# The output projection's gate rows on the weights' queue, three of them moved among the projections, and the correction turned inside a value block

## The chip, the cores and the metric

The kernel runs on one core of a Trainium2 chip. Its engines work side by side and each goes through its own list of instructions in order: TensorE (PE) multiplies matrices and loads its weights on a second track (PEld), VectorE (DVE), ScalarE (ACT) and GpSimd (POOL) compute elementwise, SyncE (SP) only issues transfers (DMAs). A DMA can also be issued by another engine, here by POOL; it then stands in that engine's list. An instruction waits until what it reads is there and what it overwrites is free.

The metric is the device time of one execution in microseconds (us); lower is better. "Before" is the kernel as it was, "after" the changed one.

## What is computed

One layer of a diffusion backbone over 512 latent tokens and 256 context tokens, model width 2048, all in float32. The lines of the reference that the change's surroundings compute:

```python
mod_x = (silu(c) @ w_ada + b_ada)                 # 6 x 2048 modulation values for the latent tokens
sh1, s1, g1, sh2, s2, g2 = split(mod_x, 6)
h = modulate(rmsnorm(x, norm1_w), sh1, s1)        # and hc for the context
p = h @ w_in                                      # one input projection: q, k, v, c_q, c_kv, k_rope
...                                               # 8 heads of differential, 8 of latent attention
x = x + g1 * (merge_heads(o_da, o_mla) @ w_o)     # output projection, 2048 x 2048, gated by g1
h2 = modulate(rmsnorm(x, norm2_w), sh2, s2)
x = x + g2 * conv_ffn(h2, w_up, conv_w, conv_b, w_down)
return rmsnorm(x, final_w)
```

The modulation `silu(c) @ w_ada` is a matrix times one vector. Its 96 rows of 128 outputs are computed apart from each other: row j brings a 128 x 2048 tile of `w_ada` (1 MB) and makes column j of the tile `modx`. Columns 0 to 31 (shift and scale of the first norm) are made at the start, 32 to 47 are the gate g1, 48 to 79 the shift and scale of the second norm, 80 to 95 the gate g2. The 64 rows behind the first 32 are spread over later stages; they are called **gate rows** here.

## The kernel before

**Products.** Each float32 product is made of three passes (`mm3`, lines 103 to 109): both operands are split into a high and a low half, and PE adds high x high (L107), high x low (L108) and low x high (L109). A weight block is a 128 x 1024 raw tile `wr` (512 KB, one DMA on SP's queue, L89 in `wraw`). ACT copies its high half `wh` out (a cast), DVE subtracts that from `wr` to give the low half `wl`, and then PE can run the block. `wh` and `wl` have three buffers each.

**A gate row** (`gemv`, L169 to L176) is a DMA of 1 MB into a tile `ada` of two buffers, and one multiply-and-sum on DVE against the activated vector held in `cb`, which writes one column of `modx`. Whatever engine `queue` names issues the DMA; without one it is SP. The rows come from one iterator `gv` in the order 64 to 79, 32 to 47, 48 to 63, 80 to 95, and `next_gemv(pool, count, queue)` takes the next `count` of them, so a row placed earlier shifts all that follow.

**The projections** (about 120 to 437 us of the span) are 36 blocks in an order written out by hand (`manual_schedule`): what the program emits in turn is what each engine does in turn. `step(block, tasks)` emits the block's matmuls, then the cast of the block two ahead, the first task, the low half of the block two ahead, the load of the block four ahead, and the other tasks. Here `wr` has two buffers. Gate rows are tasks (`gemvs(1)`) and their DMAs go on POOL's queue (`gp`); 35 of the 64 rows are done in this stage.

Eight of the blocks make the values of the first four heads (`value_block`, called for n_ = 0 to 7 with the tasks of `plan[n_]`): six products of 128 x 512, one for each group of 128 tokens, summed over 16 tiles of the width. The last of them goes through its order group by group, 12 pairs of a group and a half of the weight block.

**The correction.** The first products of the projection are made before the shift of the modulation is known, and a bias `beta` is added to them later. Two rows of sums for it are collected in two PSUM tiles `ac` (named `b_1432` and `b_1433` below); `bias_turn` turns them from rows into columns by six small products with `sel` (printed as x4 and x2), and `bias_out` copies the columns to `beta` with two DVE copies, one of 8 and one of 4 columns. Before, `bias_turn` is called after the eight value blocks, and `bias_out` is the first task of the next step, `block(1, 0)`. That step's block writes its result in PSUM.

**The output projection** (about 822 to 1027 us) is a double loop: four groups of output columns, and in each eight weight blocks of `w_o`; a block feeds four products of 128 x 512 with two tiles of the attention's output each, 24 matmuls in all. Here a scheduler orders the instructions of each engine from the program's order and the buffers: `wr` has three buffers, `ada` two, `xr` three. Behind the eighth block of a group (run in the order of the outputs) come four outputs: a tile `xr` of x is loaded on SP, DVE forms `x + g1 * product` from column 32 + dt of `modx`, POOL issues the write of the result (`x_d`) and adds its square to `ss`. Before, a gate row on POOL's queue stands ahead of each block but the first three of the first group, 29 in all:

```python
for g in range(4):
    for kb in range(8):
        if g or kb > 2:
            next_gemv(wo, 1, gp)
        wh, wl = wblock(w_o[g, kb])
        ...
    for i in range(4):
        nc.sync.dma_start(xr, x_t[dt])
        ...
        gp.dma_start(x1_d[dt], x)
```

Behind it comes the gated MLP to the end of the program; the change leaves it as it is.

Of the kernel before, what the change touches and what calls it, by code (L numbers as in the profile page):

```python
# [52 lines left out]
def layer_kernel(ctx: ExitStack, tc: tile.TileContext, small, rope, c_row, cc_row, x_t, ctx_t, ada, ada_k,  # L53
# [484 lines left out]
    def gemvs(count):  # L538
        return lambda: next_gemv(sp_, count, gp)
# [129 lines left out]

    def value_block(half, vo, n_, last):  # L670
        wh, wl = hl_w.pop(len(steps))
        order = [(j, t) for t in last for j in range(2)] if n_ == 7 else [(j, t) for j in range(2) for t in range(NKEY)]
        for j, t in order:
            kt = KB[half][n_] * 2 + j
            w = (wh[:, j * 512:(j + 1) * 512], wl[:, j * 512:(j + 1) * 512])
            src, o = (hx[kt], t * P) if t < 4 else (hc[kt], (t - 4) * P)
            mm3(vo[t], (src[0][:, o:o + P], src[1][:, o:o + P]), w, n_ == 0 and j == 0, n_ == 7 and j == 1)
# [57 lines left out]
    with tc.manual_schedule(engines=every):  # L735
        raws[4] = keep(lat0[4], None, raw_query())
        for f in (2, 3, 0, 1):
# [15 lines left out]
                [lambda: add_shift([7], gemvs(1)), gemvs(1)],  # L753
                [gemvs(1), gemvs(1)], [gemvs(1), gemvs(1)])
        for n_ in range(8):
            step(lambda: value_block(0, v0, n_, first), *plan[n_])
            if 2 < n_ < 7:
                bias_products(n_ - 3)
        bias_turn()

# [27 lines left out]

        step(block(1, 0), bias_out, lay(0), lay(5), gemvs(1), lay(1, True), gemvs(1))
        step(block(1, 1), lay(2), lay(3), gemvs(1), lay(4, True))  # L790
        step(block(2, 0), gemvs(1), feature_keys(1))
# [14 lines left out]

        step(lambda: latent(0, 0), gemvs(1))
        step(lambda: latent(0, 1), feature_keys(6))
        step(lambda: latent(1, 0), gemvs(1), lambda: keep_cq(0))
        step(lambda: latent(1, 1), gemvs(1))  # L810
        step(lambda: latent(2, 0), gemvs(1), lambda: keep_cq(1))
# [285 lines left out]
    for g in range(4):  # L1097
# [5 lines left out]
        for kb in range(8):  # L1103
            if g or kb > 2:
                next_gemv(wo, 1, gp)
            wh, wl = wblock(w_o[g, kb])
            order = [(j, i) for j in range(2) for i in range(4)]
            for j, i in sorted(order, key=lambda t: t[1]) if kb == 7 else order:
                kt, o = kb * 2 + j, j * 512 + i * P
                mm3(outs[i], (wh[:, o:o + P], wl[:, o:o + P]), osp[kt], kt == 0, kt == 15)  # L1110
# [564 lines left out]
```

## Time and profile before

| | us |
|---|---|
| three runs | 2421.64, 2428.02, 2425.93 |
| median | 2425.93 |
| the profiled execution, its own time | 2423.42 |
| its span (first to last instruction in the trace) | 2421.6 |

The mean granted clock of TensorE in the profiled execution is 0.991 of full speed.

The windows of the profile over the stages, with busy time of each engine in us (instructions in brackets), the granted clock, the share of the DMA engines and GB/s:

```profile
120.00:437.00 317.00, 311.10 (x1557) 259.51 (x1557) 248.01 (x310) 89.27 (x134) 30.77 (x57) 0.98 0.73 264
437.00:822.00 385.00, 364.11 (x1885) 285.45 (x1883) 311.92 (x495) 215.18 (x413) 40.37 (x34) 1.00 0.35 105
822.00:1027.00 205.00, 191.88 (x836) 155.26 (x837) 140.74 (x142) 56.20 (x75) 42.42 (x55) 0.98 0.74 269
1027.00:2421.00 1394.00, 1369.05 (x7494) 1191.16 (x7492) 981.42 (x1207) 688.09 (x955) 161.82 (x188) 0.99 0.52 135
```

The columns behind the length are PE, PEld, DVE, ACT and POOL. A line of the timeline, further down, reads: start, duration, engine, line, operation, output <- inputs, shapes, count, and in square brackets the time that the engine had been idle and what released it. A busy PE may still be slow: its time at a lower clock counts as busy.

### The profile page before, as it was taken

Reading aid. Unit: us, or ns where it says so; the run is one execution under the profiler, and the core shown is the slowest. Engines: PE = TensorE matmul, PEld = TensorE weight load, DVE = VectorE, ACT = ScalarE, POOL = GpSimd, SP = SyncE. Lnnn points to the kernel's source line nnn. Section 1 sums busy time; section 2 is a strip of 40 time slices with the busy share of each in tenths; the row PEclk is TensorE's granted clock in tenths of the full one; section 3 lists DMA queues with packets and bytes.
Section 4 is the critical chain, followed back from the end, with each engine's and each line's share of the span. In section 5 each row is a group of like instructions: output and inputs, shape, how many; then the busy total and the mean of one; then the engine's idle time right before and its main releaser. Section 6 shows DMA issues by size and latency. Waiting matters only on the chain.

```text
span 2421.6 us, 32339 instructions
## 1 busy us (share of the span) xinstructions
PE 2342.4 (97%) x12444; PEld 1969.0 (81%) x12444; DVE 1774.9 (73%) x2303; ACT 1099.8 (45%) x1660; POOL 281.7 (12%) x350
## 2 busy tenths in 40 slices
PE   8999999999899998999999999999999999999997
PEld 5787888777677787788888888888888888888887
DVE  5996786698787877597576767676767676676667
ACT  5322322455555621254454545454445454454543
POOL 0001000121100022200101010101011111111113
PEclk9999999999999999999999999999999999999999
DMA  9767776853301289613555454545555555555572
GB/s 381 276 225 282 289 283 257 231 151 106 127 33 48 72 324 334 213 58 130 140 134 145 129 147 124 152 120 156 122 157 122 157 122 150 129 140 138 135 213 79
DMA packets 141514, 407.45 MB, mean 168 GB/s; under 512 B 14880, under 2 KB 31792, under 8 KB 130736
## 3 DMA queue, kind: packets, MB, share of 16 engines
q1 hardware_dynamic: 103552, 271.15, 34.1%
q0 software_dynamic: 36656, 133.19, 21.2%
q8 instruction: 97, 1.59, 0.3%
q10 hardware_dynamic: 1152, 1.05, 0.1%
q14 instruction: 57, 0.47, 0.1%
HBM read 335.86 MB, written 69.48 MB: 167 GB/s over the span
## 4 chain that ended last, share of the span: by engine, by line
PE 77%; DVE 9%; issue 7%; DMA 4%; ACT 3%; POOL 2%; SPq 0%; DVEq 0%; POOLq 0%; ACTq 0%
PE y L1373 13%; PE b L107 9%; PE b L108 9%; PE b L109 9%; PE z L1373 6%; PE y L1375 6%; PE z L1375 3%; PE s L881 3%; PE x L1373 2%; PE s L108 2%; PE s L107 2%; PE s L109 2%; DMA ada<-in_ada 1%; PE x L1375 1%; PE pt L893 1%
## 5 line engine op out<-in xcount | busy, mean ns | idle before, releaser
L1394 POOL DMA_DIRECT2D x_d<-xs x160 | 140.4, 1020 | 1165.4 <-ACT xs L1393 1135.7
L107 PE MATMUL b<-ah,wh 128*128 128x512 f32 (+1 forms) x672 | 259.3, 386 | 0.0
L108 PE MATMUL b<-al,wh 128*128 128x512 f32 (+1 forms) x672 | 259.2, 386 | 0.0
L109 PE MATMUL b<-ah,wl 128*128 128x512 f32 (+1 forms) x672 | 258.3, 384 | 0.0
L1349 DVE TENSOR_TENSOR wl<-wr,wh 128x1024 fp32r<-128x1024 f32 x126 | 153.9, 1221 | 128.9 <-ACT wh L1343 128.9
L1349 DVE TENSOR_TENSOR wl<-rb,wh 128x1024 fp32r<-128x1024 f32 x124 | 151.3, 1221 | 127.8 <-ACT wh L1343 127.8
L1343 ACT CAST wh<-wr 128x1024 fp32r<-128x1024 f32 x126 | 132.2, 1049 | 206.4 <-PE b L108 100.7
L1343 ACT CAST wh<-rb 128x1024 fp32r<-128x1024 f32 x124 | 130.2, 1051 | 189.8 <-PE b L108 115.8
L1349 DVE TENSOR_TENSOR wl<-ws,wh 128x1024 fp32r<-128x1024 f32 x123 | 150.1, 1221 | 88.7 <-ACT wh L1343 88.7
L1343 ACT CAST wh<-ws 128x1024 fp32r<-128x1024 f32 x123 | 128.3, 1043 | 137.9 <-PE b L108 45.2
L174 DVE CUSTOM_DVE_ANT_0 ada<-ada,cb,smt 128x2048 f32<-128x2048 f32 x64 | 153.3, 2397 | 50.3 <-DMA ada<-in_ada 50.2
L109 PEld LDWEIGHTS b<-ah,wl 128*128 128x128 f32 x672 | 126.4, 188 | 25.5
L107 PE MATMUL b<-a2k,wh 128*128 128x512 f32 (+1 forms) x352 | 135.7, 388 | 11.0 <-DVE beta L733 5.9
L107 PEld LDWEIGHTS b<-ah,wh 128*128 128x128 f32 x672 | 126.7, 188 | 22.9
L108 PEld LDWEIGHTS b<-al,wh 128*128 128x128 f32 x672 | 126.7, 189 | 21.9
L109 PE MATMUL b<-a2k,wl 128*128 128x512 f32 (+1 forms) x352 | 134.0, 381 | 6.3 <-DVE wl L81 6.3
L80 ACT CAST wh<-wr 128x1024 fp32r<-128x1024 f32 (+2 forms) x64 | 64.0, 1002 | 120.1 <-PE s L108 37.1
L210 ACT CAST wh<-wr 128x1024 fp32r<-128x1024 f32 x38 | 39.9, 1051 | 150.4 <-PE b L109 41.9
L1373 PE MATMUL y<-b2k,wh 128*128 128x512 f32 x410 | 106.9, 391 | 0.0
L883 DVE TENSOR_REDUCE m<-s 128x1 f32<-128x768 f32 x96 | 90.4, 950 | 22.6 <-PE s L881 22.2
L1393 ACT ACTIVATE xs<-b,modx 128x512 f32<-128x512 f32 x160 | 100.8, 680 | 0.3 <-DMA x_d<-xs 0.3
L81 DVE TENSOR_TENSOR wl<-wr,wh 128x1024 fp32r<-128x1024 f32 (+2 forms) x64 | 76.4, 1196 | 30.5 <-ACT wh L80 30.4
(536 smaller groups left out, 6113.7 us busy)
## 6 DMA issues: line engine op xcount, KB each, us to landing
ada<-in_ada POOLq DMA_DIRECT2D x80, 1024.0 KB, 5.9
rb<-in_w_up SPq DMA_DIRECT2D x123, 512.0 KB, 4.4
wr<-in_w_dn SPq DMA_DIRECT2D x84, 512.0 KB, 4.0
x_d<-xs POOLq DMA_DIRECT2D x160, 256.0 KB, 6.0
wr<-in_w_up SPq DMA_DIRECT2D x53, 512.0 KB, 4.3
wr<-in_w_f SPq DMA_DIRECT2D x34, 512.0 KB, 6.1
adak<-in_ada_k SPq DMA_DIRECT2D x64, 256.0 KB, 5.4
wr<-in_w_o SPq DMA_DIRECT2D x32, 512.0 KB, 5.4
```

The lines of the kernel that those rows point to most:

```text
L81: ve.tensor_tensor(dst_l, src, dst_h.bitcast(F32), op=ALU.subtract)
L107: pe.matmul(out, st[0], mv[0], start=start, stop=False, **kw)
L108: pe.matmul(out, st[0], mv[1], start=False, stop=False, **kw)
L109: pe.matmul(out, st[1], mv[0], start=False, stop=stop, **kw)
L174: ve.tensor_tensor_reduce(out=junk, in0=w, in1=vec, op0=ALU.mult, op1=ALU.add, scale=1.0, scalar=col("b_ada", j), accum_out=dst[:, j:j + 1])
L883: ve.tensor_reduce(out=m, in_=s[:, :TT], axis=AX.X, op=ALU.max, negate=True)
L1343: sc.copy(hi, raw)
L1349: ve.tensor_tensor(lo, raw, hi.bitcast(F32), op=ALU.subtract)
L1373: pe.matmul(o, w[j][0], hs[j], start=start and j == 0, stop=False, skip_group_check=True)
L1375: pe.matmul(o[:, h0], w[j][1], hs[j][:, h0], start=False, stop=j == 7, skip_group_check=True)
L1393: sc.mul(x, po, modx[:, 80 + dt:81 + dt])
L1394: gp.dma_start(x1_d[dt], x, accum_op=ALU.add)
```

## The change

Four things are done. (a) In the output projection the gate rows lose their queue argument, so that SP issues them in between the weights' loads, and the condition changes: the first group has its rows at kb 3 to 7 as before, the three others at kb 0 to 6, none ahead of their last block. That is 5 + 3 x 7 = 26 rows. (b) The three rows taken out there become tasks of three steps of the projections, behind `block(1, 1)`, `latent(0, 0)` and `latent(1, 1)`, on POOL's queue; 38 rows are done there then. As the iterator's order stays, each place behind the first of these works on a later row than it did. (c) `bias_turn` is called in the middle of the last first-value block, after six of its 12 pairs, no longer behind it. (d) `bias_out` is emitted between the two gate rows of that block's step, no longer as the first task of the step that follows.

```diff
-    def value_block(half, vo, n_, last):
+    def value_block(half, vo, n_, last, midway=None):
...
-        for j, t in order:
+        for k, (j, t) in enumerate(order):
+            if midway and k == len(order) // 2:
+                midway()
...
-                [gemvs(1), gemvs(1)], [gemvs(1), gemvs(1)])
+                [gemvs(1), gemvs(1)], [gemvs(1), bias_out, gemvs(1)])
         for n_ in range(8):
-            step(lambda: value_block(0, v0, n_, first), *plan[n_])
+            step(lambda: value_block(0, v0, n_, first, bias_turn if n_ == 7 else None), *plan[n_])
...
-        bias_turn()
...
-        step(block(1, 0), bias_out, lay(0), lay(5), gemvs(1), lay(1, True), gemvs(1))
-        step(block(1, 1), lay(2), lay(3), gemvs(1), lay(4, True))
+        step(block(1, 0), lay(0), lay(5), gemvs(1), lay(1, True), gemvs(1))
+        step(block(1, 1), lay(2), lay(3), gemvs(1), lay(4, True), gemvs(1))
...
-        step(lambda: latent(0, 0), gemvs(1))
+        step(lambda: latent(0, 0), gemvs(1), gemvs(1))
...
-        step(lambda: latent(1, 1), gemvs(1))
+        step(lambda: latent(1, 1), gemvs(1), gemvs(1))
...
-            if g or kb > 2:
-                next_gemv(wo, 1, gp)
+            if kb != 7 if g else kb > 2:
+                next_gemv(wo, 1)
```

The three places in the instruction orders follow (a name's number counts buffers and differs between the kernels; `wl_2011` before and `wl_2017` after are the same low half).

**PE at the end of the last first-value block, before:** the last product of the block (`c2k` is the context's part, `a2k` the latent's), the turn, and the first product of `block(1, 0)`.

```order
L108 MATMUL s_1561<-wl_1893,c2k_793 128x512
L109 MATMUL s_1561<-wh_1892,c2k_794 128x512
L729 MATMUL b_1432<-sel,bias_1710 128x2 x4
L729 MATMUL b_1433<-sel,bias_1710 128x2 x2
L107 MATMUL b_2028<-a2k_367,wh_1952 128x512
L108 MATMUL b_2028<-a2k_368,wh_1952 128x512
```

The same turn after:

```order
L108 MATMUL s_1560<-wl_1893,a2k_800 128x512
L109 MATMUL s_1560<-wh_1892,a2k_801 128x512
L731 MATMUL b_1432<-sel,bias_1710 128x2 x4
L731 MATMUL b_1433<-sel,bias_1710 128x2 x2
L107 MATMUL s_1560<-wh_1892,a2k_795 128x512
L108 MATMUL s_1560<-wl_1893,a2k_795 128x512
```

The turn stands between two products of the same value block, `wh_1892`'s, and half of that block follows it.

**DVE at that block's end, before:** gate rows (L174, each with a short second instruction), low halves (L213), the copies to `beta` (L733), and `a_93`, which belongs to the second norm.

```order
L174 ISA ada_2013,modx<-ada_2013,cb,smt 128x2048
L174 ISA modx 128x1
L213 TENSOR_TENSOR wl_2011<-wr_1906,wh_2010 128x1024
L1123 SCALAR_TENSOR_TENSOR a_93<-modx,smt 128x1
L174 ISA ada_2019,modx<-ada_2019,cb,smt 128x2048
L174 ISA modx 128x1
L733 COPY beta<-b_1432 128x8
L733 COPY beta<-b_1433 128x4
L213 TENSOR_TENSOR wl_2079<-wr_1959,wh_2078 128x1024
L81 TENSOR_TENSOR kl_2087<-b_1562,kh_2086 128x512
```

After:

```order
L174 ISA ada_2019,modx<-ada_2019,cb,smt 128x2048
L174 ISA modx 128x1
L213 TENSOR_TENSOR wl_2017<-wr_1906,wh_2016 128x1024
L735 COPY beta<-b_1432 128x8
L735 COPY beta<-b_1433 128x4
L174 ISA ada_2027,modx<-ada_2027,cb,smt 128x2048
L174 ISA modx 128x1
L81 TENSOR_TENSOR kl_2084<-b_1562,kh_2083 128x512
L213 TENSOR_TENSOR wl_2081<-wr_1959,wh_2080 128x1024
L81 TENSOR_TENSOR kl_2093<-b_1563,kh_2092 128x512
```

The copies stand one gate row earlier, right behind the low half; the next low half now stands behind one `kl` of the values' split.

**SP in the output projection, where the first group ends and the second begins, before:** weights (`wr`) and the tiles `xr` of x alone.

```order
L89 DMA wr_8002<-in_w_o 128x1024
L89 DMA wr_8035<-in_w_o 128x1024
L89 DMA wr_8068<-in_w_o 128x1024
L1114 DMA xr_7954<-in_x_t 128x512
L1114 DMA xr_8230<-in_x_t 128x512
L89 DMA wr_8101<-in_w_o 128x1024
L1114 DMA xr_8238<-in_x_t 128x512
```

The rows stand on POOL there, between the writes `x_d` and the sums of squares:

```order
L171 DMA ada_7999<-in_ada 128x2048
L171 DMA ada_8032<-in_ada 128x2048
L171 DMA ada_8065<-in_ada 128x2048
L1119 DMA x_d_103<-b2k_7934 128x512
L1119 DMA x_d_104<-b2k_7940 128x512
L1080 TENSOR_TENSOR ss<-ss,sq_7943 128x512
L171 DMA ada_8098<-in_ada 128x2048
L1119 DMA x_d_105<-b2k_7948 128x512
```

SP after:

```order
L1115 DMA xr_7955<-in_x_t 128x512
L171 DMA ada_7908<-in_ada 128x2048
L171 DMA ada_7975<-in_ada 128x2048
L89 DMA wr_7978<-in_w_o 128x1024
L171 DMA ada_8008<-in_ada 128x2048
L89 DMA wr_8011<-in_w_o 128x1024
L1115 DMA xr_7963<-in_x_t 128x512
L171 DMA ada_8041<-in_ada 128x2048
L89 DMA wr_8044<-in_w_o 128x1024
```

A row now precedes each weight on SP, and POOL's list in this stage holds the writes `x_d` and the sums `ss` alone.

## The prediction

> **What bounds the kernel now.** I read the page first, then the waits of the two stages that the change touches, then the timeline of each engine at those places.
>
> ```profile
> span 2421.6 us, 32339 instructions
> PE 2342.4 (97%) x12444; PEld 1969.0 (81%) x12444; DVE 1774.9 (73%) x2303; ACT 1099.8 (45%) x1660; POOL 281.7 (12%) x350
> ```
>
> TensorE (PE) is busy for 97%, so a change can only win where PE stands still or runs at a lower clock. The waits of 114 to 440 us (the projections) and of 852 to 1020 us (the output projection) hold these rows; the columns are total us, times, longest:
>
> ```profile
> PE b L107 <- DVE beta L733: 5.9, 1, 5.9
> ...
> PE b L109 <- DVE wl L81: 6.3, 2, 5.1
> PE s L109 <- DVE wl L81: 5.8, 2, 4.5
> ...
> DVE ada L174 <- DMA ada<-in_ada: 28.8, 18, 4.8
> ```
>
> So PE waits once, 5.9 us, for the copy of the correction (`beta`), and four times, 12.1 us together, for the low half of an output-projection weight (`wl`). VectorE (DVE), which makes `wl`, itself stands 28.8 us before gate rows that have not landed. Its timeline ahead of the longest wait shows how the one makes the other; the bracket is the idle time ahead of an instruction and its releaser:
>
> ```profile
> 982.54 2.35 DVE L174 CUSTOM_DVE_ANT_0 ada<-ada,cb,smt 128x2048 f32<-128x2048 f32 x1 [4.80 <-DMA ada<-in_ada]
> ...
> 986.14 1.22 DVE L81 TENSOR_TENSOR wl<-wr,wh 128x1024 fp32r<-128x1024 f32 x1
> ```
>
> The `wl` stands behind the row in DVE's order; PE resumes 0.1 us after it. What these waits cost is on PE's timeline:
>
> ```profile
> 223.69 1.39 PE L729 MATMUL b<-sel,bias 128*128 128x2 f32 x12
> 230.99 0.80 PE L107 MATMUL b<-a2k,wh 128*128 128x512 f32 x1 [5.90 <-DVE beta L733]
> ...
> 236.25 0.28 PE L107 MATMUL b<-c2k,wh 128*128 128x256 f32 x1
> ...
> 926.50 0.50 PE L109 MATMUL s<-a2k,wl 128*128 128x512 f32 x1 [1.36 <-DVE wl L81]
> ...
> 942.21 0.50 PE L109 MATMUL s<-a2k,wl 128*128 128x512 f32 x1 [4.49 <-DVE wl L81]
> ...
> 942.77 0.63 PE L108 MATMUL s<-q2k,wh 128*128 128x512 f32 x1
> ...
> 946.18 0.39 PE L107 MATMUL s<-a2k,wh 128*128 128x512 f32 x1
> ```
>
> After the 4.49-us wait eight matmuls take 3.41 us (942.77 to 946.18), 0.43 each, where 0.227 is the pace otherwise (24 matmuls in 5.44 us, below). After the 5.90-us wait, from 230.99 to 236.25, nine 512-column and six 256-column matmuls take 5.26 us; at 0.227 and 0.114 they would take 2.7. So a long wait costs a second time: 1.6 and 2.5 us. The windows give the granted clock (the number ahead of the DMA share) behind short and long waits:
>
> ```profile
> 660.00:664.00 4.00, 1.78 (x8) 0.95 (x6) 2.28 (x4) 1.25 (x2) 0.00 (x0) 1.00 0.73 246
> 924.00:928.00 4.00, 2.64 (x12) 1.84 (x11) 3.35 (x4) 0.00 (x0) 0.53 (x1) 1.00 0.80 276
> 942.20:948.00 5.80, 5.79 (x18) 4.66 (x19) 5.80 (x5) 1.43 (x2) 1.65 (x2) 0.71 0.79 284
> 663.41 0.73 PE L881 MATMUL s<-krh,qs 128*128 128x512 f32 x2 [2.22 <-DMA krh<-kr_d]
> ```
>
> Waits of 1.36 and 2.22 us left the clock at 1.00; that of 4.49 brought 0.71.
>
> **The correction's turn.** The six turning products (12 records, 1.39 us) move into the middle of the last first-value block: the same work for PE, which comes to the next block at 225.08 as before. The copies of `beta` stand on DVE behind this:
>
> ```profile
> 225.38 1.22 DVE L213 TENSOR_TENSOR wl<-wr,wh 128x1024 fp32r<-128x1024 f32 x1
> 226.52 0.15 DVE L1123 SCALAR_TENSOR_TENSOR a<-modx,smt 128x1 f32<-128x1 f32 x1
> 228.50 2.35 DVE L174 CUSTOM_DVE_ANT_0 ada<-ada,cb,smt 128x2048 f32<-128x2048 f32 x1 [1.83 <-DMA ada<-in_ada]
> ...
> 230.77 0.23 DVE L733 COPY beta<-b 128x8 f32<-128x8 f32 x2
> ```
>
> In the new order they stand ahead of the last row and right behind the `wl` of 225.38, so they run from 226.52 to 226.75. PE then waits 1.67 us (225.08 to 226.75), not 5.90: 4.2 us won. The rest of the wait stays, because that `wl` is now late. A wait of 1.67 is nearest to those of 1.36 and 2.22, so I let the slow clock go too: 2.5 us more, **6.7** together. The ends: 4.2 if the clock drops all the same, 8.4 if nothing waits. The Trainium skill ("TensorE: Matmul & The Clock Gate", Part 1) says that the array goes to half rate after about 3.4 us of idleness and returns after as much work, which agrees with the rows above; by it the 2.5 go whole, while a loss in proportion to the wait would keep 0.7 of them.
>
> **Three rows more among the projections.** Each is 2.35 us on DVE, on POOL's queue as before. The cover is how far DVE's `wl` is ahead of PE:
>
> ```profile
> 241.92 1.05 ACT L210 CAST wh<-wr 128x1024 fp32r<-128x1024 f32 x1 [15.01 <-PE b L108]
> ...
> 243.48 0.69 DVE L81 TENSOR_TENSOR kl<-s,kh 128x512 fp32r<-128x512 f32 x1 [3.84 <-ACT kh L80]
> ...
> 257.24 0.01 DVE L153 LOAD_MASK_SELECT rt<-b  x1 [2.80 <-DMA v_d<-rt]
> ...
> 267.63 1.22 DVE L213 TENSOR_TENSOR wl<-wr,wh 128x1024 fp32r<-128x1024 f32 x1
> ...
> 275.52 1.05 ACT L210 CAST wh<-wr 128x1024 fp32r<-128x1024 f32 x1 [3.29 <-PE s L108]
> ...
> 344.73 1.22 DVE L213 TENSOR_TENSOR wl<-wr,wh 128x1024 fp32r<-128x1024 f32 x1
> ...
> 353.16 1.05 ACT L210 CAST wh<-wr 128x1024 fp32r<-128x1024 f32 x1 [3.95 <-PE b L108]
> ```
>
> A cast that waits for PE starts when a block ends and the next begins. The block that begins at 275.52 has its `wl` at 268.85, 6.7 us ahead. PE will come 6.7 us sooner, and the first added row lies ahead of this `wl`. DVE's idle 3.84 hangs on PE through the cast of 241.92 and shrinks with it; the 2.80 waits for a write that leaves sooner. They cover 2.35, but the added megabyte may make DVE wait for a row in turn. I take 0.7 us of new wait, with 0 and 3 as ends (3: the row and a fresh wait of its size less what shrinks). The two later rows meet a `wl` at 345.95 for a block at 353.16, 7.2 us, and the idle time of DVE there: nothing. This part: **-6.0** (-2.0 to -8.4).
>
> **The output projection.** Three rows fewer, and 26 loads go from POOL's queue to SyncE's (SP's), between the weight loads. PE's pace and its end are on ScalarE's casts, which start when a block ends:
>
> ```profile
> 852.31 1.06 ACT L80 CAST wh<-wr 128x1024 fp32r<-128x1024 f32 x1 [2.14 <-PE s L108]
> 857.75 1.05 ACT L80 CAST wh<-wr 128x1024 fp32r<-128x1024 f32 x1 [4.38 <-PE s L108]
> ...
> 1026.60 1.04 ACT L80 CAST wh<-wr 128x1024 fp32r<-128x1024 f32 x1 [4.39 <-PE b L108]
> ```
>
> A block is 24 matmuls, 5.44 us (852.31 to 857.75). From the end of the third block (852.31) to that of the last (1026.60) are 174.3 us for 29 blocks; at pace 157.8. So the stage loses 16.5: 12.1 of waits, about 3.2 of slow clock behind the two long ones, the rest in refilling. Is it late again in the new order? The landing times and the bytes (830 to 1000 us):
>
> ```profile
> DMA packets 11123, 52.08 MB, mean 306 GB/s; under 512 B 1311, under 2 KB 1311, under 8 KB 7273
> ...
> ada<-in_ada POOLq DMA_DIRECT2D x29, 1024.0 KB, 5.9
> wr<-in_w_o SPq DMA_DIRECT2D x26, 512.0 KB, 5.7
> xr<-in_x_t SPq DMA_DIRECT2D x15, 256.0 KB, 5.1
> cb<-silu_c SPq DMA_DIRECT2D x1, 1024.0 KB, 4.4
> 240.00:250.00 10.00, 10.00 (x58) 8.74 (x57) 5.18 (x6) 2.71 (x4) 0.36 (x2) 1.00 1.03 406
> ```
>
> DVE: a `wl` (1.2) and a row (2.35) per block are 3.6 of 5.44; a group of eight blocks, with seven rows and four outputs (0.75), takes 29 of 43.5. DMA: 49 MB in some 154 us is 318 GB/s, with 406 seen at 240 to 250. SP: a row waits for the row two before it, the weight behind it then needs 5.9 + 1.05 + 1.2 us, 8.2 at most, against the two blocks (10.9) that it is issued ahead. A row's own loop over two buffers is 5.9 + 2.35 + 0.33 (SP's issue) = 8.6 us for two rows, under 10.9. The tight place is the end of the first group. Block 9 begins at 852.31 + 6 x 5.44 = 884.9; its `wl` stands behind the fourth output, whose `xr` is issued after the first output at about 877.5. With 5.1 it lands at 882.6, and 0.75 + 1.2 later the `wl` is there at 884.5: just in time. A landing of 8 us would make it about 3 late. At later group ends the `wl` of two blocks ahead is already made. I take **-16.5**; ends -13 and -16.5.
>
> Sum: 2423.4 (the profiled execution) - 6.0 - 16.5 = 2400.9. That execution is 2.5 below the median of the three runs (2425.93; 2421.64 to 2428.02), so for a median I say **2402**.
>
> **Rivals.** (1) *The bytes bound the stage, not the order.* Then only the three rows that leave help, 3/29 of 16.5 = 1.7: 2423.4 - 6.0 - 1.7 = 2416. For it: landings of 5.9 us beside a `cb` of the same size in 4.4. Against: 306 GB/s where 406 were reached. The Trainium skill ("DMA: Bandwidth & Descriptors", Rules for kernel authors) speaks for this rival: spreading transfers over issuing engines brings no bandwidth, as all run on the same 16 engines; by it the move from one queue to another is worth nothing in itself, and no run here shows the move yet. (2) *SP's order holds the weights back: slower.* A row may take up to 2 x 5.44 - 2.7 = 8.2 us to land before its loop over two buffers sets the pace. If row and weight land strictly one after the other (5.9 + 5.7 = 11.6), a block takes (11.6 + 2.7) / 2 = 7.15, 1.7 too long; 26 times is 44: 2423.4 - 22.5 + 44 = 2445. It is slower than before from a landing of about 9.9 on. For it: 8.34 occurs, below. Against: that one lay between two queues at work.
>
> ```profile
> 974.07 8.34 DMA ada<-in_ada
> ```
>
> (3) *DVE is the bound among the projections too.* The rows then give back the 6.0, and a late group end costs 3: 2423.4 - 13.5 = 2410. (4) *Both fall short* (1 and 3 together): 2422, no change.
>
> **How the numbers follow.** A measurement of this kernel can tell about 0.3% (7.3 us) from no change, so faster means under 2418.6. Forecast (2396 to 2406) 0.68, rival 3 (to 2413) 0.13, rival 1 (to 2418) 0.07, rival 4 0.07, rival 2 0.05. Range: 2396 (8.4 and 16.5 won, less 2 of scatter) to 2413. Faster 0.87, same 0.08, slower 0.05.
>
> **What would show it.** In the profile of the changed kernel: a wait of PE for `beta` of about 1.7 us with the clock at 1.00; no wait of PE for `wl` over 1 us between 840 and 1010; 157 to 161 us over the same 29 blocks. Wrong: casts in that stage that wait for `wr` landings at every block (rival 2), DVE still standing tens of us before rows with PE behind it (rival 1), or a new wait for `wl` near 269 us (rival 3).

## The result and the profile after

| | before | after |
|---|---|---|
| median of four runs each, us | 2423.78 (2419.19 to 2428.02) | 2407.32 (2403.86 to 2411.65) |
| ratio | | 0.9933, 95% interval 0.9907 to 0.9959 |
| the profiled execution, us | 2423.42 | 2411.65, the slowest of its four |

The kernel became 16.5 us faster at the median where 24 were forecast. A second series (below) gave 2410.8 against 2427.3, 16.5 again.

The page of the kernel after, span and first busy row:

```profile
span 2409.9 us, 32334 instructions
PE 2343.0 (97%) x12444; PEld 1969.4 (82%) x12444; DVE 1775.9 (74%) x2303; ACT 1101.1 (46%) x1660; POOL 274.1 (11%) x324
```

The waits of PE among the projections (114 to 420 us), and the waits of VectorE (DVE) in the output projection (840 to 1010 us); total us, times, longest:

```profile
PE b L107 <- DVE beta L735: 3.8, 1, 3.8
PE b L296 <- ACT row L290: 2.9, 1, 2.9
PE b L109 <- DVE wl L213: 0.2, 1, 0.2
```

```profile
DVE ada L174 <- DMA ada<-in_ada: 15.8, 14, 2.2
```

From 840 to 1010 us PE's waits for `wl`, 12.1 us before, are gone, and DVE's for rows have fallen from 28.8 to 15.8. The windows of that stretch, before and then after, say the same: PE is busy throughout, at full granted clock, while the transfers move no faster (the last column is GB/s).

```profile
840.00:1010.00 170.00, 157.88 (x682) 129.01 (x681) 121.35 (x114) 42.25 (x53) 40.26 (x51) 0.98 0.83 304
```

```profile
840.00:1010.00 170.00, 170.00 (x757) 140.59 (x756) 122.76 (x115) 48.21 (x59) 31.13 (x23) 1.00 0.79 301
```

Four casts on ScalarE's timeline divide the span of the kernel after: the last of L399, the 36th of L210, and the two between which 29 blocks of the output projection lie.

```profile
130.01 0.72 ACT L399 CAST wh<-wr 128x640 fp32r<-128x640 f32 x1
...
411.35 1.06 ACT L210 CAST wh<-wr 128x1024 fp32r<-128x1024 f32 x1 [7.10 <-PE b L109]
...
854.84 1.05 ACT L80 CAST wh<-wr 128x1024 fp32r<-128x1024 f32 x1 [2.14 <-PE s L108]
...
1012.60 1.04 ACT L80 CAST wh<-wr 128x1024 fp32r<-128x1024 f32 x1 [4.38 <-PE b L108]
```

Before they stand at 129.28, 413.09, 852.31 and 1026.60. So the 11.7 us between the two spans are: start +0.7, projections 283.8 to 281.3 (-2.5), attention 439.2 to 443.5 (+4.3), the 29 blocks 174.3 to 157.8 (-16.5), what follows +2.3. The output projection lost all that was forecast; the projections won 2.5 where 6.0 were forecast, and the stages that the change doesn't touch lost 7.3. Which of this is the change, and which is one execution, is what the experiments had to show.

### The profile page after: what moved, and what is told of

Read it like the earlier page. It is cut to its first block, busy times and chain, and to the rows that moved or that the text cites. A ratio compares the mean times of both kernels' runs of the same rounds, so it can differ in the third digit from the quotient of the medians.

```text
span 2409.9 us, 32334 instructions
## 1 busy us (share of the span) xinstructions
PE 2343.0 (97%) x12444; PEld 1969.4 (82%) x12444; DVE 1775.9 (74%) x2303; ACT 1101.1 (46%) x1660; POOL 274.1 (11%) x324
## 4 chain that ended last, share of the span: by engine, by line
PE 75%; issue 10%; DVE 9%; ACT 3%; DMA 2%; POOL 1%; SPq 0%; DVEq 0%; POOLq 0%; ACTq 0%
PE y L1374 12%; PE b L107 8%; PE b L108 8%; PE b L109 8%; PE z L1374 6%; PE y L1376 6%; PE z L1376 3%; PE s L882 3%; PE x L1374 2%; PE s L108 2%; PE s L109 2%; PE s L107 2%; PE x L1376 1%; PE pt L894 1%; PE f L107 1%
## 5 line engine op out<-in xcount | busy, mean ns | idle before, releaser
L174 DVE CUSTOM_DVE_ANT_0 ada<-ada,cb,smt 128x2048 f32<-128x2048 f32 x64 | 154.3, 2414 | 56.7 <-DMA ada<-in_ada 56.6
L108 PEld LDWEIGHTS b<-al,wh 128*128 128x128 f32 x672 | 126.6, 188 | 21.9
L210 ACT CAST wh<-wr 128x1024 fp32r<-128x1024 f32 x38 | 40.0, 1052 | 131.4 <-DMA wr<-in_w_f 49.4
```

Of the source, the lines that this page charges most:

```text
L108: pe.matmul(out, st[0], mv[1], start=False, stop=False, **kw)
L174: ve.tensor_tensor_reduce(out=junk, in0=w, in1=vec, op0=ALU.mult, op1=ALU.add, scale=1.0, scalar=col("b_ada", j), accum_out=dst[:, j:j + 1])
```

## The experiments

Each kernel is compared, by the ratio of the times, with runs of the kernel before on the same chip. "The 29 blocks" and "the projections" are the distances between the casts above, from one profiled execution each.

**The queue alone, at the old places.** Edit to the kernel before:

```diff
             if g or kb > 2:
-                next_gemv(wo, 1, gp)
+                next_gemv(wo, 1)
```

> The kernel before with one edit: the output projection's gate rows lose their queue argument; all 29 keep their places, so SP issues them between the weights. Theory (the queue and the order in it did it: on one queue each row arrives before the weight behind which DVE needs it): the 29 blocks take 157 to 161 us where before took 174.3 and after 157.8, PE waits under 1 us in all for wl there, and the time falls by 13 to 17 us. Rival A (the places did it: no row ahead of a group's last block, and three rows fewer): the 29 blocks stay at 170 us or more, waits for wl of 1 to 5 us stay at the group ends, and the time falls by 4 us at most. Rival B (SP's order holds weights back with a row at every block): over 176 us, slower than before.

Measured: 2410.06 us against 2427.26, ratio 0.9926 (0.9912 to 0.9939). No wait of PE from 840 to 1010 us, and the 29 blocks, timeline of ScalarE:

```profile
855.96 1.05 ACT L80 CAST wh<-wr 128x1024 fp32r<-128x1024 f32 x1 [2.14 <-PE s L108]
...
1013.72 1.04 ACT L80 CAST wh<-wr 128x1024 fp32r<-128x1024 f32 x1 [4.38 <-PE b L108]
```

157.8 us, at PE's pace with all 29 rows. The whole gain of the change in this stage is here: rivals A and B fall, and with the rows on SP their places and number in the program add nothing to it. The time fell by 17.2 us, the upper end of the theory's 13 to 17.

The gain is not that anything came sooner. From 840 to 1010 us DVE waited 27.1 us for rows, where before it waited 28.8, and the casts on ScalarE waited more for weights than before (21.9 us, 5 times):

```profile
ACT wh L80 <- DMA wr<-in_w_o: 79.1, 20, 10.5
```

In this window the median from issue to landing is 7.2 us for a row, 8.1 for a weight and 7.6 for an x tile, where before it was 6.3, 5.9 and 5.1. So the sign that the prediction named for its rival 2, casts that wait for weights, is there 20 times, without its loss: the low halves were still ready when PE came to them.

**The new places, on POOL's queue.** Edit to the kernel after:

```diff
             if kb != 7 if g else kb > 2:
-                next_gemv(wo, 1)
+                next_gemv(wo, 1, gp)
```

> The changed kernel with the 26 rows of the output projection on POOL's queue as they were before; places, count, the three rows among the projections and the correction's turn as in the changed kernel. Theory (the queue): most of the waits come back; only the last group's end, where the row at kb 7 was the one waited for, is freed (5.1 us of wait and 1.6 of slow clock), so the 29 blocks take 164 to 170 us and the time is 6 to 12 us over the changed kernel's 2407. Rival A (places and count): 157 to 161 us for the 29 blocks, time within 3 us of the changed kernel's.

Measured: 2414.54 us, ratio 0.9943 (0.9926 to 0.9959). The 29 blocks took 167.8 us, as the theory said; the time did not follow it. It is 3.8 us over the changed kernel's 2410.78 in the same series, where the theory said 6 to 12 and rival A at most 3, and the intervals of the two ratios (0.9928 for the changed kernel, below) overlap, so the time doesn't decide. The profiled execution had no wait for `beta` at all, and its projections took 277.0 where the changed kernel's took 281.3. What waits came back is on DVE's timeline; this is the longest, with PE's wait behind it:

```profile
934.57 0.75 DVE L1117 SCALAR_TENSOR_TENSOR b2k<-b,modx,xr 128x512 f32<-128x512 f32 x1 [7.96 <-DMA xr<-in_x_t]
```

```profile
936.51 0.80 PE L109 MATMUL s<-a2k,wl 128*128 128x512 f32 x1 [6.66 <-DVE wl L81]
```

It is not a row that DVE stands for, but a tile of x (`xr`), with the low half behind it. The same was so in the kernel before, ahead of the 4.49-us wait of PE at 942.21:

```profile
940.27 0.75 DVE L1116 SCALAR_TENSOR_TENSOR b2k<-b,modx,xr 128x512 f32<-128x512 f32 x1 [5.42 <-DMA xr<-in_x_t]
940.94 1.22 DVE L81 TENSOR_TENSOR wl<-wr,wh 128x1024 fp32r<-128x1024 f32 x1
```

From 860 to 1030 us DVE waited for `xr` 9.1 us before and 15.8 here, with the rows on POOL, and 2.0 after and 2.9 with the queue alone.

**The correction's turn alone.** The kernel before with `midway`, `bias_turn` in the last block and `bias_out` between its two rows, as in the change, and nothing else.

```diff
-        bias_turn()
...
-                [gemvs(1), gemvs(1)], [gemvs(1), gemvs(1)])
+                [gemvs(1), gemvs(1)], [gemvs(1), bias_out, gemvs(1)])
...
-        step(block(1, 0), bias_out, lay(0), lay(5), gemvs(1), lay(1, True), gemvs(1))
+        step(block(1, 0), lay(0), lay(5), gemvs(1), lay(1, True), gemvs(1))
```

> The kernel before with the correction's turn and its copies alone moved, nothing else. PE waited 5.9 us for beta before and 3.8 in the profile of the changed kernel, where 1.7 was forecast. Theory (the wait that is left is the two gate rows that stand ahead of the copies on DVE and whose landing times scatter by some us from one execution to the next): a wait of 1 to 4 us, its size given by the idle time of DVE ahead of these two rows, and a time 2 to 6 us under before. Rival (the three added rows, which come later in the program, made the projections dearer): here the wait is 1.7 or less and the time falls by 6 us or more.

Measured: 2423.62, ratio 0.9976 (0.9960 to 0.9991). The wait of PE:

```profile
PE b L107 <- DVE beta L735: 1.7, 1, 1.7
```

1.7 us, the size forecast, and the projections took 277.5 us, 6.3 less than before. In the 2 us behind the wait the granted clock (the third number from the end) is 1.00, where it was 0.50 before (230.99 to 232.99 us), so the slow clock went too, as the prediction assumed:

```profile
226.63:228.63 2.00, 2.00 (x11) 1.74 (x12) 1.92 (x2) 0.86 (x2) 0.00 (x0) 1.00 0.78 205
```

The time fell by 3.6 us by the medians and by 5.8 by the ratio (2 to 10 by its interval), so it doesn't decide between the two sides. The output projection, here as in the kernel before, lost more in this execution: 179.6 us for the 29 blocks, where PE waited 13.6 us for `wl`.

**The changed kernel once more.**

> The changed kernel once more, for a second profile and more runs. Theory: 2402 to 2412 us; the output projection's 29 blocks take 157 to 160 us again, since nothing waits there; PE's wait for beta differs from 3.8 by a us or more, since it hangs on the landing of two rows; and the loss of 3.3 us at 660 to 680 us of the span (granted clock 0.65 and 0.84 there, 1.00 in the profile of before) is gone or there again whatever the change, as it follows a wait for krh in a stage that the change doesn't touch. Rival (that loss is the change's doing): it is there again, and in none of the kernels with the old output projection.

Measured: 2410.78, ratio 0.9928 (0.9913 to 0.9944); the 29 blocks 158.3. PE's waits from 114 to 445 us, and a window behind the wait for `krh`:

```profile
PE b L107 <- DVE beta L735: 6.0, 1, 6.0
PE s L882 <- DMA ks<-k_d: 5.0, 1, 5.0
```

```profile
670.00:680.00 10.00, 8.40 (x29) 6.82 (x30) 4.74 (x8) 2.22 (x5) 0.00 (x0) 0.66 0.11 32
```

The wait for `beta` is 6.0 this time, in the same code that had 3.8, and 0 in the kernel with the rows on POOL. And the slow clock behind `krh` is there again, so this run alone can't tell scatter from an effect of the change; the other profiles do (last section).

**The copies one row earlier still.** Edit to the kernel after:

```diff
-                [gemvs(1), gemvs(1)], [gemvs(1), bias_out, gemvs(1)])
+                [gemvs(1), gemvs(1)], [bias_out, gemvs(1), gemvs(1)])
```

> The changed kernel with the copies to beta one gate row earlier still: first task of that step, so ahead of the low half and of both its rows. In three profiles of the changed projections PE waited 3.8, 6.0 and 0 us for beta, as the row ahead of the copies landed late or not; where it waited 3.8 or 6.0 the granted clock fell to 0.71 and 0.64 behind it. Theory: DVE passes the copies at about 224 us of the span, before PE asks for them at about 226, so no wait for beta is left, and the time falls by 3 to 6 us against the changed kernel (ratio to before about 0.991 where the changed kernel has 0.993). Rival (PE then waits as long for the next low half or row, since DVE is the bound there): wait for wl of over 2 us between 225 and 260 us, and no gain.

Measured: ratio 0.9920 (0.9903 to 0.9938), not told apart from the changed kernel's 0.9928. No wait for `beta`, but waits for `wl`, as the rival had it, though they come later than its 225 to 260 us. PE's two, and DVE's timeline ahead of the first:

```profile
262.67 0.50 PE L109 MATMUL b<-a2k,wl 128*128 128x512 f32 x1 [1.93 <-DVE wl L213]
274.80 0.79 PE L109 MATMUL b<-a2k,wl 128*128 128x512 f32 x1 [3.45 <-DVE wl L213]
```

```profile
259.12 2.35 DVE L174 CUSTOM_DVE_ANT_0 ada<-ada,cb,smt 128x2048 f32<-128x2048 f32 x1 [4.44 <-DMA ada<-in_ada]
261.39 1.22 DVE L213 TENSOR_TENSOR wl<-wr,wh 128x1024 fp32r<-128x1024 f32 x1
```

The projections took 284.4 us, no less than before (283.8). With PE on time for `beta`, DVE is late some blocks further on: for the first wait behind a row that had to land, for the second (its `wl` starts at 273.53) behind its own work, which runs without a pause from 267.59 on and has a row of 2.35 us in it.

**Without the three added rows; and that with the early copies.** Edit to the kernel after (the second kernel takes the edit above too):

```diff
-        step(block(1, 1), lay(2), lay(3), gemvs(1), lay(4, True), gemvs(1))
+        step(block(1, 1), lay(2), lay(3), gemvs(1), lay(4, True))
...
-        step(lambda: latent(0, 0), gemvs(1), gemvs(1))
+        step(lambda: latent(0, 0), gemvs(1))
...
-        step(lambda: latent(1, 1), gemvs(1), gemvs(1))
+        step(lambda: latent(1, 1), gemvs(1))
...
-            if kb != 7 if g else kb > 2:
+            if g or kb > 2:
                 next_gemv(wo, 1)
```

> The changed kernel without the three added rows among the projections: the correction's turn as changed, and all 29 rows of the output projection on SP at the places they had before. Rows on SP alone gave 2410.1 us, the changed kernel 2410.8, the turn alone 2423.6 (before 2427.3). Theory (the three rows take back what the turn wins, as DVE waits longer for rows among the projections: 40.7, 34.7 and 48.4 us with them, 21.4, 23.5 and 34.4 without): 2404 to 2408 us, ratio to before 0.990 to 0.992, DVE's wait for rows from 120 to 437 us under 36. Rival (the three rows cost nothing, the turn itself wins nothing, and e3's gain is scatter): 2410 or more, ratio 0.993 or more.

> The kernel of e6_no_three (turn moved, 29 rows on SP, no row added among the projections) with the copies to beta as early as in e5_copy_early. Theory (both effects add): no wait for beta, output projection at 157 to 161 us for its 29 blocks, 2401 to 2406 us, ratio to before 0.989 to 0.991, the fastest of all. Rival (they win the same time, since either is enough to take the wait): as e6_no_three within 2 us.

Measured: 2404.77, ratio 0.9907 (0.9885 to 0.9929), and 2407.29, ratio 0.9909 (0.9891 to 0.9927). From 114 to 420 us PE waits only for `row` (L296, 2.8 and 2.9 us, a wait that all these kernels have) and once for a low half (0.6 and 0.9 us). Neither kernel waits for `beta`. The projections took 275.4 and 276.6 us, the 29 blocks 157.8 in both. The first has the best median of all that was run, 22.4 us under before, and lies in its theory's 2404 to 2408; DVE waited 28.3 us for rows from 120 to 437 us, where the theory said under 36 and the changed kernel had 40.7 and 48.4. Its interval overlaps the changed kernel's. The early copies add nothing to it (the rival of the second, whose theory, 2401 to 2406, fails).

**Two of the three rows.** Edit to the kernel after: the row behind `block(1, 1)` goes back to the end of the output projection.

```diff
-        step(block(1, 1), lay(2), lay(3), gemvs(1), lay(4, True), gemvs(1))
+        step(block(1, 1), lay(2), lay(3), gemvs(1), lay(4, True))
...
-            if kb != 7 if g else kb > 2:
+            if kb != 7 if 0 < g < 3 else g or kb > 2:
                 next_gemv(wo, 1)
```

> The changed kernel without the first of the three rows added among the projections (the one behind the block that begins near 250 us); that row goes back to the last block of the last group in the output projection, on SP. The changed kernel gave 2410.8 us, none of the three rows 2404.8. Theory (the first row costs, since it stands ahead of the low half near 269 us; the two later ones lie in idle time of DVE): 2403 to 2407 us, ratio to before 0.990 to 0.992, and no wait of PE for wl over 1 us from 250 to 290 us. Rival (the rows cost by their bytes or number, whichever they are): 2408 to 2411, ratio 0.992 to 0.9935.

Measured: 2407.97, ratio 0.9902 (0.9882 to 0.9922). By the median it is on the border of the two, by the ratio with the theory, and PE's waits from 114 to 420 us hold none for `wl` and almost none for `beta`:

```profile
PE b L107 <- DVE beta L735: 0.2, 1, 0.2
```

The projections took 276.0 us, as without any of the three, in the fastest of its six executions (2401.17). That the first row is the one that costs is what the profiles show (below, where the prediction is answered); by the time it is likely, not settled, as the interval overlaps the changed kernel's.

**The rows among the projections on SP's queue too.** Edit to the kernel after:

```diff
     def gemvs(count):
-        return lambda: next_gemv(sp_, count, gp)
+        return lambda: next_gemv(sp_, count)
```

> The changed kernel with the rows among the projections on SP's queue as well, at the places where they are written. Theory (one queue helps where the row is asked for before the weight and nothing else stands in the queue; here SP also carries the writes of keys and values, which wait for results, and rows and weights behind these start late): PE waits more for weights' halves, and the time is 5 to 40 us over the changed kernel. Rival (one queue is better wherever rows and weights meet): DVE's wait for rows from 120 to 437 us falls under 25 us and the time is 3 us or more under the changed kernel.

Measured: 2523.37, ratio 1.0389 (1.0369 to 1.0409), 96 us slower than before: far beyond the theory's 5 to 40 us, on its side. The waits on SP's queue and of PE, from 120 and 114 to 540 us:

```profile
SPq L89 <- DVE wl L213: 203.7, 34, 11.5
SPq L555 <- ACT kh L562: 44.4, 9, 10.7
```

```profile
PE b L109 <- DVE wl L213: 36.3, 13, 8.3
PE b L108 <- DVE wl L213: 20.9, 5, 8.7
PE b L107 <- DVE beta L735: 14.2, 1, 14.2
```

SP stands 204 us until a low half frees a buffer for the next weight (L89), and 44 us before writes of keys (L555) whose data is not there. Most of this is not new: in the changed kernel the same two waits are 158.2 and 37.6 us. New is that the rows stand behind them in SP's list. They are asked for late, not carried slowly: a row takes 5.9 us from issue to landing here and in the changed kernel (medians, 120 to 540 us). DVE waits for them 159 us (21 to 48 in the other kernels), and its low halves, which free the buffers that SP waits for, come late in turn.

**Queue or order on DVE?** Moving the rows to SP had changed a second thing. The scheduler had also given DVE another order: with POOL's queue two rows stood ahead of a low half at eight places, with SP's a row and a low half took turns, but for the first group, where low halves ran further ahead and two rows stood ahead of one and three ahead of another. DVE's timeline before:

```profile
919.13 2.35 DVE L174 CUSTOM_DVE_ANT_0 ada<-ada,cb,smt 128x2048 f32<-128x2048 f32 x1 [2.79 <-DMA ada<-in_ada]
922.95 2.35 DVE L174 CUSTOM_DVE_ANT_0 ada<-ada,cb,smt 128x2048 f32<-128x2048 f32 x1 [1.46 <-DMA ada<-in_ada]
925.23 1.22 DVE L81 TENSOR_TENSOR wl<-wr,wh 128x1024 fp32r<-128x1024 f32 x1
```

Three kernels, each the kernel before but for the output projection's order, wrote DVE's order out and left the other engines to the scheduler. Two took turns, low halves two blocks ahead, one with `gp` and one without:

```diff
+    ahead_ = [wblock(w_o[0, i]) for i in range(2)]
+    with tc.manual_schedule(engines={mybir.EngineType.DVE}):
...
             if g or kb > 2:
                 next_gemv(wo, 1, gp)
-            wh, wl = wblock(w_o[g, kb])
+            if i_ + 2 < 32:
+                ahead_.append(wblock(w_o[(i_ + 2) // 8, (i_ + 2) % 8]))
+            wh, wl = ahead_.pop(0)
```

The third followed the old order instruction by instruction (g a row, L a low half, B an output), on SP:

```diff
+    seq = ("L0 L1 L2 L3 L4 g L5 g L6 g g L7 g L8 g g B0 B1 L9 g B2 B3 L10 g L11 g L12 g g L13 g L14 g L15 g g L16 g L17 "
+           "B4 g B5 B6 B7 L18 g g L19 L20 g g L21 g L22 g g L23 g L24 g g B8 B9 L25 g B10 B11 L26 L27 L28 L29 L30 L31 "
+           "B12 B13 B14 B15")
```

> The kernel before with only the output projection's order on DVE written out: low halves two blocks ahead of PE and one gate row ahead of each (five in the first group, eight in the others, 29 in all), where before DVE had two rows in a row ahead of a low half at eight places; the rows stay on POOL's queue. The move to SP's queue (e1_rows_sp) had changed two things at once: the queue, and with it the order that the scheduler gave DVE. Theory A (the queue itself: separate queues bring row and weight late in turn, whatever DVE's order): the 29 blocks take 168 us or more, PE waits 5 us or more for wl, and e10_sp_order, which has the same order on DVE, is 10 us or more faster. Theory B (DVE's order: two rows ahead of a low half): the 29 blocks take 157 to 162 us here too, the time is 2409 to 2415 us, and within 4 us of e10_sp_order.

> As e9_pool_order, with the same order on DVE, but the 29 rows on SP's queue. Both theories: 157 to 161 us for the 29 blocks and 2408 to 2413 us, as in e1_rows_sp; it is the other half of the pair with e9_pool_order.

> The fourth corner of the square: the kernel before with the output projection's order on DVE written out as it was before (two rows ahead of a low half at eight places), and the 29 rows on SP's queue. So far the 29 blocks took 174.3 and 179.6 us (POOL, old order), 162.5 (POOL, one row per low half), 157.8 (SP, either of two orders with about one row per low half). Theory (DVE's order is the larger part, since the low half must wait for two rows whichever queue brings them): 165 to 175 us for the 29 blocks, waits of PE for wl of 5 us or more in all, ratio to before 0.995 to 1.000. Rival (one queue is enough, since the rows land in the order in which DVE asks and the loop over two buffers has slack): 157 to 161 us, ratio to before 0.992 to 0.9935.

The medians were 2420.91 and 2413.09 us for the two with turns (before 2430.76), and 2422.12 for the third (before 2427.20). The square, ratio to before (interval) and the 29 blocks of one profiled execution:

| DVE's order | rows on POOL | rows on SP |
|---|---|---|
| two rows ahead of a low half | 1; 174.3 us (179.6 with the turn alone) | 0.9979 (0.9965 to 0.9993); 164.3 us |
| a row and a low half in turn | 0.9955 (0.9938 to 0.9972); 162.5 us | 0.9930 (0.9912 to 0.9948); 157.8 us |

Each profile is one execution: the third kernel's, 2416.0 us, was the fastest of its runs (median 2422.1), those of the two with turns, 2425.7 and 2419.1, the slowest of theirs. The order with turns also puts the four outputs of a group together, which the old one did not, so what the square varies is the whole order, not the pairs of rows alone. What PE still waited for from 840 to 1010 us, first with the turns on POOL, then with the old order on SP:

```profile
PE b L109 <- DVE wl L81: 2.9, 1, 2.9
```

```profile
PE b L109 <- DVE wl L81: 1.7, 2, 0.9
PE s L109 <- DVE wl L81: 1.3, 1, 1.3
PE s L107 <- ACT wh L80: 1.0, 1, 1.0
PE b L107 <- ACT wh L80: 0.4, 1, 0.4
```

The third kernel came out near its theory (4.4 us of waits and 164.3 us where 5 and 165 were the lower ends; the ratio within). But of the two pure theories neither stands. Theory A fails, since turns on POOL already take 12 of the 16.5 us from the 29 blocks; Theory B fails, since the queue makes a further 4.7 us and 0.0025 of the time; and one queue is not enough either. By the ratios the order alone is worth 0.45% (0.28 to 0.62), the queue alone 0.21% (0.07 to 0.35), both 0.70%. How the queue gains its part with DVE's order held fixed stays open. The wait left on POOL is again that for an x tile: DVE's timeline shows

```profile
987.33 0.75 DVE L1121 SCALAR_TENSOR_TENSOR b2k<-s,modx,xr 128x512 f32<-128x512 f32 x1 [6.54 <-DMA xr<-in_x_t]
```

5.3 us ahead of the one wait of PE, at 992.61.

## Why the prediction was right, and where it missed

The time of 2407.3 us lies in the stated range of 2396 to 2413, but in the part that the prediction gave to rival 3 (2406 to 2413) and not in its forecast of 2402. The gain of 16.5 us is the size of the output projection's term alone; that of the projections came to about nothing by the ratios.

**The output projection: right in size, half right in cause.** -16.5 was forecast for the 29 blocks, and 174.3 became 157.8 (158.3 in the second profile, 157.8 with the queue alone). The forecast gave the cause as the `wl` standing behind a row in DVE's order. By the middle values of the square DVE's order is the larger part, though the intervals overlap; but the step spoke of the move to SP's queue as the edit that does it, and did not see that the queue also changed the order on DVE, nor that one of the four waits that it counted, that of 4.49 us, came from a late x tile.

**Rival 1** (the bytes bound the stage, so only three rows less can help): refuted by the queue alone, with all 29 rows, at PE's pace. The Trainium skill ("DMA: Bandwidth & Descriptors", Rules for kernel authors) was right that another issuing engine brings no bandwidth: 304 and 301 GB/s from 840 to 1010 us. It does not follow that the move is worth nothing, since what was short was not bandwidth but the order in which things arrive and are asked for. **Rival 2** (SP holds the weights back) cost nothing here, though weights did land later on SP's queue (8.1 us against 5.9). Among the projections SP's order made the program 96 us slower than before; there the rows came late, behind loads and writes that wait in the same queue.

**The turn: right on average.** A wait of 1.67 us for `beta` was forecast. Six profiles have the copies at the new place (without the one with all rows on SP): 3.8, 6.0, 0, 1.7, 0 and 0.2 us, 1.95 in the mean. The five with the old place and a profile like before's show 5.9, 6.4, 6.7, 5.2 and 6.0. The term of 6.7 us fits too: the projections took 283.3 to 285.4 us in these five (284.2 in the mean) and 277.5 and 275.4 with the copies at the new place and no row added, 7.7 less. The term was given as one number, though, while it hangs on the landing of two rows and scatters from 0 to 6 us. In the kernel after they landed late; DVE's timeline, where before the second began at 223.10:

```profile
220.90 2.35 DVE L174 CUSTOM_DVE_ANT_0 ada<-ada,cb,smt 128x2048 f32<-128x2048 f32 x1 [2.25 <-DMA ada<-in_ada]
...
226.09 2.35 DVE L174 CUSTOM_DVE_ANT_0 ada<-ada,cb,smt 128x2048 f32<-128x2048 f32 x1 [2.64 <-DMA ada<-in_ada]
...
229.50 0.23 DVE L735 COPY beta<-b 128x8 f32<-128x8 f32 x2
```

**The three rows: the step that missed.** "I take 0.7 us of new wait, with 0 and 3 as ends." Without them the changed kernel runs at 0.9907 instead of 0.9928, about 5 us; so the -6.0 for the two edits among the projections came to about nothing by the ratios (queue alone 0.9926, queue with turn and rows 0.9928), while turn and queue without the rows gave 22.4 us where the terms 6.7 and 16.5 make 23.2. The profiles show where it goes. The projections take 277.5, 275.4 and 276.6 us with the turn and no added row, 276.0 with the two later ones, and 281.3, 284.3, 277.0 and 284.4 with all three. In the first two of these the loss is the wait for `beta` (3.8 and 6.0 us with the slow clock behind it), in the last it is the 5.4 us of waits for `wl`. For the wait for `beta` the added rows are no cause that the program shows, since up to the copies its instructions are the same with and without them; that these two executions fell to the late side may be chance.

What the first added row does is the same in all four profiles that have it on POOL's queue. In DVE's order three rows now stand between two low halves where two stood, and DVE has to wait for the third. After, where the low half started at 252.61 before:

```profile
258.37 2.35 DVE L174 CUSTOM_DVE_ANT_0 ada<-ada,cb,smt 128x2048 f32<-128x2048 f32 x1 [4.04 <-DMA ada<-in_ada]
...
260.65 1.22 DVE L213 TENSOR_TENSOR wl<-wr,wh 128x1024 fp32r<-128x1024 f32 x1
```

That wait is 4.04, 3.34, 4.00 and 4.44 us in the four, and the low half starts at 256.5 to 262.8; in the four with the turn and without this row it starts at 250.5 to 251.5. So the fresh wait on DVE, for which the prediction allowed at most the row's own 2.35 us, is 3.3 to 4.4, and it comes one low half earlier than the one near 269 us that it looked at. What PE pays depends on whether it is late itself: 0.2 and 0.4 us for `wl` in the two executions that had already waited for `beta`, 1.0 and 5.4 in the two that had not. This is Rival 3, DVE as the bound there. The 5 us, whose intervals overlap, are thus part row and part scatter of the wait for `beta`, and the runs don't divide them.

Two sums of the prediction don't come out: with 4.2 won and 3 lost the lower end of -6.0 is -1.2, not -2.0, and 2400.9 plus the 2.5 of the median is 2403.4, not 2402.

**What lies outside the terms.** The attention and what follows lost 6.6 us in the profiled execution. No run ties this to the change: over 13 profiles (all but the one with all rows on SP) the stretch between the second and third cast takes 438.7 to 448.9 us, and both 438.7 and 447.6 in kernels whose projections are the same. The profile of before was at the low end (439.2), and its base was the fixed point of the whole sum.

## What to carry to other kernels

Read a wait of the bound engine one step further back than its releaser: here `wl` was late because its engine stood in order before a load, and moving that load to another queue also made the scheduler write that engine's order anew; hold one of the two fixed before saying which did it. Put loads on one queue in the order in which one consumer asks for them, and look first at what else in that queue waits, for results or for a free buffer: the same edit won 17 us in one stage and cost 113 in another (2523.4 us against the changed kernel's 2410.8). A single wait that hangs on landing times is a spread, not a number; look at several profiles before summing it.

## What the runs showed of the hardware

The prediction read "waits of 1.36 and 2.22 us left the clock at 1.00" as a rule. PE's wait for `krh` near 660 us stands in the same 13 profiles with 1.77 to 3.16 us, and up to 1.14 more for the next load within 2 us. In four the granted clock stayed at 1.00, in nine it fell to between 0.50 and 0.71 in one of the next 3-us windows. Neither the lengths nor the change separates the two groups: among the four are the queue alone and the new places on POOL, among the nine three kernels whose projections are those of before (the square's). The wait, and the windows behind it, with the queue alone, and then with the early copies and no added row:

```profile
666.54 0.73 PE L881 MATMUL s<-krh,qs 128*128 128x512 f32 x2 [2.02 <-DMA krh<-kr_d]
667.98 0.47 PE L881 MATMUL s<-krlz,qs 128*128 128x512 f32 x1 [0.71 <-DMA krlz<-kr_d]
```

```profile
666.54:669.54 3.00, 2.29 (x13) 1.80 (x14) 0.46 (x1) 0.00 (x0) 0.00 (x0) 1.00 0.22 74
669.54:672.54 3.00, 1.76 (x10) 1.32 (x9) 2.66 (x6) 1.87 (x4) 0.00 (x0) 1.00 0.00 0
```

```profile
657.13 0.73 PE L882 MATMUL s<-krh,qs 128*128 128x512 f32 x2 [2.12 <-DMA krh<-kr_d]
658.18 0.47 PE L882 MATMUL s<-krlz,qs 128*128 128x512 f32 x1 [0.32 <-DMA krlz<-kr_d]
```

```profile
657.13:660.13 3.00, 2.68 (x11) 2.14 (x12) 0.50 (x1) 0.00 (x0) 0.00 (x0) 0.76 0.16 56
660.13:663.13 3.00, 2.42 (x9) 1.84 (x9) 2.20 (x4) 1.98 (x4) 0.00 (x0) 0.50 0.00 0
```

2.73 us of waiting left the clock alone, 2.44 halved it. The Trainium skill ("TensorE: Matmul & The Clock Gate", Part 1) says that the activity window is free-running, so that the same kernel meets it at different phases; that agrees with the spread. Its advice ("Why this matters for your kernels"), "No PE-idle gaps >~3µs between matmul bursts", is no safe bound here: shorter gaps dropped the clock in eight of the nine. What one such drop costs is seen behind 662 us after, where the clock was 0.50 to 0.70 for 12 us: from the wait for `krh` to PE's wait for `wth` (703.44; before 700.91) the same work took 41.0 us, before at full clock 37.5. These 3.5 us are most of the 4.3 that the attention lost.
